# 784 more matmul pairs on zeros behind the warm-up of a two-block transformer kernel

## The chip, the cores and the metric

The kernel runs on one core of a Trainium2 chip. The metric is the device time of one execution in microseconds. Before the change the median of two runs is 2268.91 us (2268.64 to 2269.18).

## What is computed

The reference applies two transformer blocks, one after the other, to 256 tokens of width 2048, in float32. Cut to what matters:

```python
h = x
hn = rms_norm(h, norm_mix[i])
h = h + nsa_mixer(hn, nsa_w_in[j], nsa_w_out[j], ...)
hn = rms_norm(h, norm_ffn[i])
h = h + jnp.square(jax.nn.relu(hn @ ffn_w1[i])) @ ffn_w2[i]
gate = jax.nn.sigmoid(rms_norm(h, norm_ple[i]) @ ple_w_gate[i])
h = h + (p[i] @ ple_w_proj[i]) * gate
x = rms_norm(h, norm_final)
...
h = rms_norm_2(x, norm_g[i, 0])
m = swa_sink_attention(h, swa_w_in[j], swa_w_out[j], swa_sinks[j], rel_bias_table)
x = x + rms_norm_2(m, norm_g[i, 1])
h = rms_norm_2(x, norm_g[i, 2])
x = x + rms_norm_2(conv_ffn(h, ffn_w_up[i], ffn_conv[i], ffn_w_down[i]), norm_g[i, 3])
```

Nearly all of the work is products of the 256 tokens with weights, some 400 MB of them, each read once.

## The kernel before

The weights come as one stream of 128 x 128 blocks, in the order in which they are used. Class `Weights` loads 16 blocks (1 MB) at a time into one of three `w_raw` buffers (lines 216 to 231) and splits 8 blocks at a time into one of four `w_split` buffers (lines 233 to 249): ScalarE writes a rounded high part (line 243), VectorE the rest as a low part (line 244), both in the float32r type that TensorE takes in one pass. A load goes out when both halves of the buffer's last content are split, and a split into a buffer waits until TensorE has read what stood there.

A product to float32 accuracy is then three products of high and low parts. There are two forms of it. In `mm` (lines 297 to 303) the weight block is stationary: a matmul of the high part with 512 columns (the tokens' high and low parts side by side, line 302), then one of the low part with 256 columns (line 303). This is the pair that the change is about. In `mm_rows` (lines 316 to 325) the tokens are stationary, and 512 columns of weights stream past: three matmuls (lines 323, 324, 325) for each half of the tokens. Each matmul instruction loads its own stationary operand first; the trace has these loads as PEld.

All stationary operands of the float32r matmuls start at a multiple of 256 bytes within a partition; tiles named `pad` take up what is needed for that. The one exception is the warm-up's tile `idle`, which starts 224 bytes past such a multiple.

The program starts in `build` (from line 452): loads of the tokens and of the first weights, then a warm-up of nine matmuls of 512 columns on the zeros of `idle` (lines 485 to 489), whose output nobody reads. Then, for each of the 16 tiles of tokens, a split of the tile (line 500, done in lines 355 and 356) and its part of the first product (line 503, `mm_rows`); lines 543 and 544 follow with a second product of the same kind. The first `mm` is on line 554. The programs of the engines are written out in the order in which a tile framework's scheduler places them; it also sets the waits between engines. The engines are TensorE (PE), VectorE (DVE), ScalarE (ACT), GpSimd (POOL) and SyncE (SP, which issues the loads).

Of the kernel before, what the change touches and what calls it, by code (L numbers as in the profile page):

```python
# [8 lines left out]
F32 = mybir.dt.float32  # L9
F32R = mybir.dt.float32r  # L10
# [3 lines left out]
P = 128  # L14
S = 256
# [250 lines left out]
class Program:  # L266
# [185 lines left out]
    def build(self):  # L452
        tc, nc, ins = self.tc, self.nc, self.ins
        self.base = tc.alloc_tile_pool(name="base", bufs=1)
        self.psum = tc.alloc_tile_pool(name="psum", bufs=1, space=bass.MemoryType.PSUM)
        self.dram = tc.alloc_tile_pool(name="dram", bufs=1, space=bass.MemoryType.DRAM)
        self.pad(self.base, 64)
        self.w = Weights(nc, self.base, ins["w"], self.blocks)

        self.vecs = self.tile(self.base, [P, NV], F32, "vecs")  # L460
        cst = self.tile(self.base, [P, NC_], F32, "cst")
        self.ident = cst[:, C_ID : C_ID + P]
        self.ones = cst[:, C_ONE : C_ONE + P]
        self.fold = cst[:, C_FOLD : C_FOLD + 64]
        self.mask = cst[:, C_MASK : C_MASK + S]
        self.cmask = cst[:, C_CMASK : C_CMASK + 32].rearrange("p (b n) -> p b n", b=2)
        self.cvalid = cst[:, C_CVALID : C_CVALID + 32].rearrange("p (b n) -> p b n", b=2)

        self.eps = self.tile(self.base, [P, 1], F32, "eps")
        nc.vector.memset(self.eps, EPS)  # L470
        nc.scalar.dma_start(self.vecs[:, :KD], ins["vec"][:, :KD])
        self.x_pool = x_pool = tc.alloc_tile_pool(name="x0", bufs=1, side="right")
        x0 = [self.tile(x_pool, [P, 2, S], F32, f"x{i}") for i in range(KD // 2)]

        def load_x(i):
            nc.sync.dma_start(x0[i], ins["x"][:, 2 * i : 2 * i + 2])

        self.w.load(W_RAW, load_x)
        for i in range(2 * W_RAW, KD // 2):
            load_x(i)  # L480
        nc.scalar.dma_start(cst, ins["cst"])
        nc.scalar.dma_start(self.vecs[:, KD:], ins["vec"][:, KD:])


        idle = self.tile(x_pool, [P, COLS], F32R, "idle")
        nc.vector.memset(idle.bitcast(F32), 0.0)
        ps = self.ps_mm()
        for i in range(WARM):
            nc.tensor.matmul(ps, lhsT=idle[:, :P], rhs=idle, start=True, stop=True)


        xs = []
        acc = self.tile(x_pool, [P, S], F32, "acc")
        self.ps_vs = [self.ps_att(), self.ps_att()]
        for k in range(KD):
            src = x0[k // 2][:, k % 2]
            if k % 2 == 0:
                self.w.split(k // 2 + 1)
            x = self.slot(k, F32R)
            self.split512(x, src, self.vec(V_MIX + k))  # L500
            self.add_square(acc, src, k == 0)
            xs.append(x)
            self.mm_rows(self.ps_vs, [x], k == 0, k == KD - 1)
        self.pad(self.base, 96)
        self.nsa(xs, acc)
        self.ffn()
        self.ple()
        self.swa()
        self.conv_ffn()
        for pool in (self.pool_z, self.pool_y, self.dram, self.psum, self.base):  # L510
            pool.release()
        assert self.w.at == self.blocks

    def band_bias(self):

        nc, ins = self.nc, self.ins
        pool = self.tc.alloc_tile_pool(name="band", bufs=1)
        table = self.tile(pool, [BUCKETS, SWA_HEADS], F32, "table")
        hot = self.tile(pool, [BUCKETS, 2 * BANDP], F32, "hot")
        nc.sync.dma_start(table, ins["table"])  # L520
        nc.sync.dma_start(hot, ins["band"])
        ps = self.ps_att()
        nc.tensor.matmul(ps[:SWA_HEADS, :BANDP], lhsT=table, rhs=hot[:, :BANDP], start=True, stop=True)
        rows = self.tile(pool, [SWA_HEADS, BANDP], F32, "rows")
        nc.vector.tensor_tensor(rows, ps[:SWA_HEADS, :BANDP], hot[:, BANDP:], op=ALU.add)
        self.band = self.tile(self.dram, [SWA_HEADS, COPIES, BANDP], F32, "bandd")
        for c in range(0, COPIES, 16):
            nc.sync.dma_start(self.band[:, c : c + 16], rows[:, None, :].to_broadcast([SWA_HEADS, 16, BANDP]))
        pool.release()
# [690 lines left out]
```

## Time and profile before

| | |
|---|---|
| median of two runs | 2268.91 us |
| the profiled execution | 2269.81 us |
| its span, first to last instruction | 2268.0 us |
| PE busy | 2236.1 us (99%) |
| DVE busy | 1447.1 us (64%) |
| ACT busy | 1181.1 us (52%) |
| POOL busy | 243.2 us (11%) |
| HBM read | 410.03 MB |

The times of an instruction are those of the hardware's profiler. Matmuls are pipelined and their ends are modelled, so what one costs in a stream is read from the distance between starts, not from its duration. The granted clock is the share of TensorE's full clock that was granted. For the first 10 us the column of the clock prints full speed where the distances are those of half speed; there the distances are used.

### The profile page before, as it was taken

How to read it: one execution, taken by the hardware profiler on the slowest of the kernel's cores; microseconds unless marked ns; L12 is line 12 of the kernel's file. 1: busy time of each engine (PE TensorE's matmuls, PEld its weight loads, DVE VectorE, ACT ScalarE, POOL GpSimd, SP SyncE). 2: the span in 40 equal slices, each digit the busy share in tenths (PEclk: the TensorE clock that was granted, in tenths of full speed). 3: DMA queues.
4: the chain of work that ended last, by engine and by line, in shares of the span. 5: the costliest groups of instructions: out<-in, count | busy, mean ns of one | idle time of the engine just before them, and what ended most of it. 6: DMA issues, size and time to landing. Idle time of an engine off the chain costs nothing. (4 is left out here: it accounts for less than half of the span.)

```text
span 2268.0 us, 29986 instructions
## 1 busy us (share of the span) xinstructions
PE 2236.1 (99%) x11645; PEld 1892.5 (83%) x11645; DVE 1447.1 (64%) x2181; ACT 1181.1 (52%) x1894; POOL 243.2 (11%) x309
## 2 busy tenths in 40 slices
PE   8999999999999999999999999999999999999998
PEld 6888887888888888888888888778888888888886
DVE  7676665566544566644566777567756766765775
ACT  4566554444433444444465566456545544554554
POOL 5432210000000000000001123002100100110110
PEclk9999999999999999999999999999999999999999
DMA  6553335555555555555555544445555555555553
GB/s 254 196 199 127 123 128 213 185 201 186 196 192 191 197 186 187 186 186 188 212 191 185 204 142 165 167 147 189 187 195 189 188 186 186 186 189 200 186 186 130
DMA packets 65950, 415.64 MB, mean 183 GB/s; under 512 B 7408, under 2 KB 12528, under 8 KB 17424
## 3 DMA queue, kind: packets, MB, share of 16 engines
q1 hardware_dynamic: 65376, 413.01, 50.5%
q8 instruction: 91, 1.49, 0.2%
q10 hardware_dynamic: 432, 0.73, 0.1%
q14 instruction: 51, 0.42, 0.0%
HBM read 410.03 MB, written 3.67 MB: 182 GB/s over the span
## 5 line engine op out<-in xcount | busy, mean ns | idle before, releaser
L244 DVE TENSOR_TENSOR w_split<-w_raw,w_split 128x1024 fp32r<-128x1024 f32 (+1 forms) x759 | 946.4, 1248 | 641.9 <-ACT w_split L243 636.4
L243 ACT ACTIVATE w_split<-w_raw 128x1024 fp32r<-128x1024 f32 (+1 forms) x759 | 801.6, 1057 | 699.4 <-PE att L325 447.9
L302 PE MATMUL mm<-slot,w_split 128*128 128x512 f32 x3152 | 1117.3, 399 | 1.5 <-DVE z L346 1.5
L303 PE MATMUL mm<-slot,w_split 128*128 128x256 f32 x3152 | 885.2, 281 | 0.0
L302 PEld LDWEIGHTS mm<-slot,w_split 128*128 128x128 f32 x3152 | 592.0, 188 | 149.8 <-issue 3.4
L303 PEld LDWEIGHTS mm<-slot,w_split 128*128 128x128 f32 x3152 | 595.3, 189 | 0.3
L324 PE MATMUL att<-w_split,h 128*128 128x512 f32 x848 | 330.2, 389 | 0.0
L325 PE MATMUL att<-w_split,h 128*128 128x512 f32 x848 | 330.2, 389 | 0.0
L323 PE MATMUL att<-w_split,h 128*128 128x512 f32 x848 | 330.1, 389 | 0.0
L344 ACT ACTIVATE t<-mm 128x256 f32<-128x256 f32 x201 | 76.4, 381 | 228.5 <-PE mm L303 227.0
L325 PEld LDWEIGHTS att<-w_split,h 128*128 128x128 f32 x848 | 159.2, 188 | 33.1
L324 PEld LDWEIGHTS att<-w_split,h 128*128 128x128 f32 x848 | 159.2, 188 | 32.9
L323 PEld LDWEIGHTS att<-w_split,h 128*128 128x128 f32 x848 | 159.2, 188 | 32.8
L1107 POOL TENSOR_TENSOR u<-z,rb 128x256 f32<-128x256 f32 x88 | 71.0, 808 | 694.3 <-DVE z L346 585.3
L346 DVE TENSOR_TENSOR z<-mm,t 128x256 f32<-128x256 f32 x201 | 84.8, 423 | 79.8 <-ACT t L344 79.8
L324 PE MATMUL att<-w_split,slot 128*128 128x512 f32 x320 | 125.9, 393 | 4.0 <-DVE w_split L244 3.9
L323 PE MATMUL att<-w_split,slot 128*128 128x512 f32 x320 | 125.2, 393 | 1.8 <-ACT w_split L243 1.7
L325 PE MATMUL att<-w_split,slot 128*128 128x512 f32 x320 | 125.7, 393 | 0.0
L919 POOL MEMSET vh<- 128x512 f32 x1 | 0.5, 524 | 910.1 <-DVE sum L391 910.1
L324 PEld LDWEIGHTS att<-w_split,slot 128*128 128x128 f32 x320 | 60.4, 189 | 19.2 <-DVE w_split L244 6.8
L323 PEld LDWEIGHTS att<-w_split,slot 128*128 128x128 f32 x320 | 60.3, 189 | 15.1 <-ACT w_split L243 3.0
L325 PEld LDWEIGHTS att<-w_split,slot 128*128 128x128 f32 x320 | 60.4, 189 | 12.2
(261 smaller groups left out, 1901.0 us busy)
## 6 DMA issues: line engine op xcount, KB each, us to landing
w_raw<-in_w SPq DMA_DIRECT2D x376, 1024.0 KB, 4.8
bias<-bandd SPq DMA_DIRECT2D x32, 128.0 KB, 2.7
w_raw<-in_w SPq DMA_DIRECT2D x5, 512.0 KB, 7.6
x<-in_x SPq DMA_DIRECT2D x8, 256.0 KB, 6.9
slot<-in_xn SPq DMA_DIRECT2D x8, 256.0 KB, 7.9
gain<-in_rows SPq DMA_DIRECT2D x2, 1024.0 KB, 6.1
out<-slot SPq DMA_DIRECT2D x8, 256.0 KB, 2.0
bandd<-rows SPq DMA_DIRECT2D x2, 768.0 KB, 6.4
```

Of the source, the lines that this page charges most:

```text
L243: nc.scalar.activation(hi[:, c], raw[:, c], AF.Copy)
L244: nc.vector.tensor_tensor(lo[:, c], raw[:, c], hi[:, c].bitcast(F32), op=ALU.subtract)
L302: nc.tensor.matmul(ps, lhsT=hi, rhs=x, start=i == 0, stop=False)
L303: nc.tensor.matmul(ps[:, S:], lhsT=lo, rhs=x[:, :S], start=False, stop=i == n - 1)
L323: nc.tensor.matmul(ps[b], lhsT=xh, rhs=hi, start=first and i == 0, stop=False)
L324: nc.tensor.matmul(ps[b], lhsT=xh, rhs=lo, start=False, stop=False)
L325: nc.tensor.matmul(ps[b], lhsT=xl, rhs=hi, start=False, stop=last and i == n - 1)
L344: nc.scalar.activation(t, ps[:, S : 2 * S], AF.Copy)
L346: nc.vector.tensor_tensor(z, ps[:, :S], t, op=ALU.add)
L919: nc.gpsimd.memset(t[:, :, :, 64:128].bitcast(F32), 0.0)
L1107: nc.gpsimd.tensor_tensor(u[:, 2:], self.total(ps), rb, op=ALU.mult)
```

## The change

Behind the warm-up a function `probe` is called. It makes two tiles of zeros, `pa` with 1024 and `pc` with 512 columns, and issues 56 groups of 14 pairs. A pair has the two shapes of lines 302 and 303: 512 columns, then 256, each with a stationary operand of its own, the first cut from the left half of `pa`, the second from the right. Within a group both keep their place: `hi` and `lo` columns of four bytes past a multiple of 128 columns, so 0, 32, ... 224 bytes past a multiple of 512 (both tiles start at a multiple of 256 bytes in the built program). The groups run over all 56 pairs of different places. The multiple changes from pair to pair in a cycle of three. Nobody reads the output.

```diff
         for i in range(WARM):
             nc.tensor.matmul(ps, lhsT=idle[:, :P], rhs=idle, start=True, stop=True)
+        self.probe()
...
+    def probe(self):
+
+        nc = self.nc
+        pool = self.tc.alloc_tile_pool(name="probe", bufs=1)
+        a = self.tile(pool, [P, 1024], F32R, "pa")
+        c = self.tile(pool, [P, 512], F32R, "pc")
+        nc.vector.memset(a.bitcast(F32), 0.0)
+        nc.vector.memset(c.bitcast(F32), 0.0)
+        for hi in range(0, 64, 8):
+            for lo in range(0, 64, 8):
+                if hi == lo:
+                    continue
+                ps = self.ps_mm()
+                for i in range(14):
+                    at = P * (i % 3)
+                    nc.tensor.matmul(ps, lhsT=a[:, at + hi : at + hi + P], rhs=c, start=True, stop=True)
+                    at += 512
+                    nc.tensor.matmul(ps[:, :S], lhsT=a[:, at + lo : at + lo + P], rhs=c[:, :S], start=True, stop=True)
+        pool.release()
```

PE's queue at the program's start, before; the matmuls of lines 323 to 325 are those of the first product:

```order
L489 MATMUL mm_14_102<-idle_13_100 128x512 x9
L323 MATMUL att_16_113<-w_split0_115,slot0_18_120 128x512
L323 MATMUL att_17_114<-w_split0_115,slot0_18_120 128x512
L324 MATMUL att_16_113<-w_split0_115,slot0_18_120 128x512
L325 MATMUL att_16_113<-w_split0_115,slot0_18_120 128x512
```

The same with the change: the warm-up, the first pairs of the first group, and the last pairs of the last with what follows them.

```order
L489 MATMUL mm_14_102<-idle_13_100 128x512 x9
L530 MATMUL mm_17_119<-pc_16_116,pa_15_115 128x512
L532 MATMUL mm_17_119<-pc_16_116,pa_15_115 128x256
...
L530 MATMUL mm_72_1714<-pc_16_116,pa_15_115 128x512
L532 MATMUL mm_72_1714<-pc_16_116,pa_15_115 128x256
L323 MATMUL att_74_1745<-w_split0_1747,slot0_76_1752 128x512
L324 MATMUL att_74_1745<-w_split0_1747,slot0_76_1752 128x512
L325 MATMUL att_74_1745<-w_split0_1747,slot0_76_1752 128x512
```

All 1568 matmuls stand between the warm-up and the first product, and but for a few swapped neighbours in the first product PE's queue is unchanged behind them.

ACT's queue in the first product, before; `slot8` to `slot15` are tiles of tokens, `w_split4` is the fifth split of weights, the first that has to wait for a buffer that PE releases:

```order
L243 ACTIVATE w_split3_132<-w_raw1_86 128x1024 [waits DMAHW3_49]
L355 ACTIVATE slot8_33_238<-x4_9_76,vecs_2_64 128x256 [waits DMAHW4_49]
L355 ACTIVATE slot9_35_255<-x4_9_76,vecs_2_64 128x256
L243 ACTIVATE w_split4_161<-w_raw2_91 128x1024 [waits DMAHW5_49,DVE_49,PE_49]
L355 ACTIVATE slot10_37_267<-x5_10_77,vecs_2_64 128x256 [waits DMAHW6_49]
L355 ACTIVATE slot11_39_282<-x5_10_77,vecs_2_64 128x256
L243 ACTIVATE w_split5_188<-w_raw2_91 128x1024 [waits DMAHW7_49,DVE_49,PE_49]
```

The same with the change:

```order
L243 ACTIVATE w_split3_1764<-w_raw1_86 128x1024 [waits DMAHW3_49]
L355 ACTIVATE slot8_91_1870<-x4_9_76,vecs_2_64 128x256 [waits DMAHW4_49]
L355 ACTIVATE slot9_93_1887<-x4_9_76,vecs_2_64 128x256
L355 ACTIVATE slot10_95_1899<-x5_10_77,vecs_2_64 128x256 [waits DMAHW6_49]
L355 ACTIVATE slot11_97_1914<-x5_10_77,vecs_2_64 128x256
...
L355 ACTIVATE slot15_105_1970<-x7_12_79,vecs_2_64 128x256
L243 ACTIVATE w_split4_1793<-w_raw2_91 128x1024 [waits DMAHW5_49,DVE_49,PE_49]
L243 ACTIVATE w_split5_1820<-w_raw2_91 128x1024 [waits DMAHW7_49,DVE_49,PE_49]
```

The fifth and sixth split now stand behind all tiles of tokens, on ACT and in the same way on DVE. The queues of POOL and SP are unchanged.

## Rows read from the trace of the kernel before

**Rows 1.** The page's first part: busy time, share of the span, instructions.
```profile
PE 2236.1 (99%) x11645; PEld 1892.5 (83%) x11645; DVE 1447.1 (64%) x2181; ACT 1181.1 (52%) x1894; POOL 243.2 (11%) x309
```

**Rows 2.** PE's waits, 0 to 60 us: total us, times, longest.
```profile
PE att L324 <- DVE w_split L244: 3.9, 5, 1.7
PE att L323 <- ACT w_split L243: 1.7, 1, 1.7
```

**Rows 3.** Stretches of the start: busy us and instructions of each engine.
```profile
core 0: us, PE busy (x) PEld busy (x) DVE busy (x) ACT busy (x) POOL busy (x), PEclk, DMA share, GB/s
1.48:7.44 5.96, 4.21 (x10) 2.81 (x10) 0.51 (x2) 2.42 (x3) 1.18 (x2) 1.00 0.87 251
7.44:59.04 51.60, 47.52 (x196) 36.90 (x197) 39.92 (x35) 26.00 (x35) 32.61 (x29) 1.00 0.70 263
```

**Rows 4.** Line 489, the warm-up: ns min/median/max, first and last start in us.
```profile
L489 PEld LDWEIGHTS mm<-idle x9: 286/330/333, 1.5 to 4.6; 128*128 128x128 f32 x9
L489 PE MATMUL mm<-idle x9: 628/628/793, 1.5 to 5.1; 128*128 128x512 f32 x9
```

**Rows 5.** Timeline of PE from 7.4 us: start us, us, instruction, idle before.
```profile
7.44 1.22 PE L323 MATMUL att<-w_split,slot 128*128 128x512 f32 x2 [1.75 <-ACT w_split L243]
...
8.46 0.33 PEld L325 LDWEIGHTS att<-w_split,slot 128*128 128x128 f32 x1
8.88 0.63 PE L325 MATMUL att<-w_split,slot 128*128 128x512 f32 x1
9.31 0.63 PE L324 MATMUL att<-w_split,slot 128*128 128x512 f32 x1
...
10.16 0.47 PE L323 MATMUL att<-w_split,slot 128*128 128x512 f32 x1
10.47 0.40 PE L324 MATMUL att<-w_split,slot 128*128 128x512 f32 x1
10.70 0.40 PE L325 MATMUL att<-w_split,slot 128*128 128x512 f32 x1
```

**Rows 6.** Timeline of PE, 512-column matmuls in a row: first and last of seven.
```profile
700.50 0.39 PE L324 MATMUL att<-w_split,h 128*128 128x512 f32 x1
...
701.86 0.39 PE L324 MATMUL att<-w_split,h 128*128 128x512 f32 x1
```

**Rows 7.** Timeline of PE, end of the first two products.
```profile
58.68 0.50 PE L376 MATMUL att<-cst,acc 128*128 128x2 f32 x4
59.04 0.48 PE L302 MATMUL mm<-slot,w_split 128*128 128x512 f32 x1
```

**Rows 8.** Timeline of DVE, its first long instructions.
```profile
0.94 0.48 DVE L486 MEMSET idle<- 128x512 f32 x1
6.26 0.48 DVE L356 SCALAR_TENSOR_TENSOR slot<-x,vecs,slot 128x256 fp32r<-128x256 f32 x1 [4.83 <-ACT slot L355]
```

**Rows 9.** Timeline of PE, pairs of lines 302 and 303: first and eighteenth.
```profile
559.82 0.40 PE L302 MATMUL mm<-slot,w_split 128*128 128x512 f32 x1
...
565.83 0.40 PE L302 MATMUL mm<-slot,w_split 128*128 128x512 f32 x1
```

**Rows 10.** A stretch at the lower clock; the columns are those of rows 3.
```profile
1512.20:1519.00 6.80, 5.84 (x24) 5.37 (x25) 6.76 (x15) 3.15 (x8) 0.00 (x0) 0.50 0.01 2
```

**Rows 11.** Timeline of PE in that stretch: two pairs' first matmuls.
```profile
1517.27 0.63 PE L312 MATMUL mm<-slot,w_split 128*128 128x512 f32 x1
...
1517.91 0.63 PE L312 MATMUL mm<-slot,w_split 128*128 128x512 f32 x1
```

**Rows 12.** Timeline of PE, a change from 64 to 128 rows.
```profile
1288.18 0.28 PE L972 MATMUL att<-kt,q 64*128 64x256 f32 x1
1288.39 0.50 PE L302 MATMUL mm<-slot,w_split 128*128 128x512 f32 x1
1288.73 0.28 PE L303 MATMUL mm<-slot,w_split 128*128 128x256 f32 x1
```

## The prediction

> **What bounds the kernel now.** I read the page's first part, then the waits of TensorE (PE), then the stretches by engine, and only then single rows. The first part says that PE has a matmul in flight for 2236.1 of 2268.0 us, 99% of the span, VectorE (DVE) 64%, ScalarE (ACT) 52% [rows 1]. Of the waits of its first 60 us behind the warm-up there are only two kinds, 3.9 and 1.7 us, both for the split of the first weights [rows 2]. So the end is set by PE's own queue, instruction after instruction. A matmul put into that queue costs its own spacing, except where it falls into a stretch in which PE would have stood still. That leaves two questions: how much standing still there is at the place of the change, and how long one added pair takes.
>
> **The place.** The stretches show the start in two pieces [rows 3]: from 1.48 us the nine warm-up matmuls and a gap, and from 7.44 to 59.04 the first 192 real matmuls (two products of 96, lines 323 to 325). The added pairs stand in PE's queue between the ninth warm-up matmul and the first real one. The warm-up's last matmul starts at 5.1 us [rows 4], and at that clock one takes its 512 columns in 0.43 us (8.88 to 9.31 in the real ones [rows 5]), so a pair could start at 5.5 us. The first real matmul starts at 7.44, waiting for ACT [rows 5]: 1.94 us of cover.
>
> More cover lies behind. The 192 real matmuls and four small ones take 51.60 us [rows 3]. In a full stretch a 512-column matmul starts every 0.2267 us: 700.50 to 701.86 is six of them [rows 6]. 192 x 0.2267 = 43.53 us, and the four small ones of line 376 take 0.36 (58.68 to 59.04 [rows 7]). The remaining 7.71 us of the 51.60 are waits for the first weights and matmuls at the lower clock. After the pairs, hundreds of microseconds later, the first four split buffers, all sixteen activation tiles and the next three loads lie ready, so I take all of it as saved. Together the cover is 1.94 + 7.71 = 9.65 us.
>
> That ACT and DVE now split the activations before the fifth weight buffer, as the order shows, costs nothing: the fifth split waits for PE to release the first buffer. Behind it on ACT stand only further splits. PE eats one buffer in 12 x 0.2267 = 2.72 us and has four, so the fifth is wanted 8.2 us after it can be begun. If that cover were gone, a wait as long as the longest one now, 1.7 us [rows 2], would come back. The two new memsets on DVE follow that of the warm-up, which took 0.48 us for 512 columns [rows 8]. Three times that ends near 2.9 us, under the warm-up, and ahead of DVE's next work at 6.26 [rows 8]. Nothing else moves: SP's and POOL's queues are as they were, and so is every fixed address from the first projection on, but for buffers that rotate.
>
> **What one pair costs.** 56 groups of 14 are 784 pairs: one matmul of 512 columns and one of 256, each with weights of its own. The kernel has such pairs already, lines 302 and 303: from 559.82 to 565.83 us there are 17, so 0.3535 us a pair [rows 9]. All of their stationary operands start at place 0, a multiple of 256 bytes. In the probe the two start at two different places out of eight, 32 bytes apart. The trace before has no such pair at the full clock. So it has to be bounded.
>
> - From below: at the lower clock (granted 0.50, the level of 1.2 GHz) a pair takes 0.64 us: 1517.27 to 1517.91 [rows 10, 11]. There no overhead shows. Half of that, 0.320 us, is what the columns alone take at 2.4 GHz. 784 x 0.320 = 250.9 us.
> - From above: behind matmuls that use 64 rows, a 256-column one holds PE for 0.21 us (1288.18 to 1288.39) and the next 512-column one for 0.34 (to 1288.73) [rows 12]: 0.55 in place of 0.3535, as where a weight load isn't hidden. 784 x 0.55 = 431.2 us.
> - The only stationary that is off place in matmuls of this type is the warm-up's, 224 bytes past a multiple of 256 in the built program. At the lower clock its weight loads took 330 ns [rows 4], as the real ones did in the same stretch (0.33 [rows 5]), and no loss showed.
>
> Between ends far apart I take the row of the same two shapes at the same clock, 0.3535: 784 x 0.3535 = 277.1 us. The six 0.2267 rows (with 0.1133 for 256 columns, 0.340) would give 266.6.
>
> The Trainium skill, TensorE: Matmul & The Clock Gate, section Back-to-back issue gap, has a rule that speaks against this value: warm, a matmul starts columns / 2.4 + 2.5 ns after the one before. By it a pair is 325 ns and the sum 254.8 us. Here the trace doesn't agree: it has 227 ns [rows 6] where the rule has 216, and 353.5 [rows 9] where it has 325.
>
> **The clock.** The first pairs run at the lower level: the spacing is still 0.43 us at 9.31, and 0.23 from 10.47 on [rows 5]. PE did nothing from 5.5 to 7.44. With the pairs it is busy throughout, so I expect the rise between 5.5 and 10.3. Each microsecond at the lower level loses 1 - 0.3535/0.64 = 0.45 us: none to 2.15 us, I take 1.1.
>
> **The sum.** 277.1 + 1.1 - 9.65 = 268.6 us more. The profiled execution took 2269.81 us, span and what lies around it, 0.9 above the median of 2268.91, so the sum applies to either. On the median it gives 2537.5 us, 11.8% slower. About 2%, 45 us, is what a measurement of this kernel can tell from no change; the first 27 pairs (9.65 / 0.3535) are covered, and from some 155 on the loss passes 2%.
>
> **Rivals.**
> - *Off-place weights are dearer.* A load that starts between two multiples of 256 touches one stretch more, and the next matmul waits for it. For it: 33.5 ns of each pair are already more than its columns. Against: no loss in the warm-up, though only at the lower clock. With that overhead doubled a pair takes 0.387 us: 303.4 + 1.1 - 9.65 = 294.9, 2563.8 us. At the upper bound it is 422.7 more, 2691.6.
> - *Different places are cheaper.* The overhead comes from both loads falling on the same place, and goes where they differ. For it: loads of all kinds in the trace before share place 0, and all show overhead. Against: 512-column matmuls in a row have 13 ns of it and a pair 33.5, with the same places. With none left: 250.9 + 1.1 - 9.65 = 242.4, 2511.3 us. The page's rule named above would come out near there, at 2515.
> - *Zeros don't raise the clock.* For it: it rose 2.9 us after the first real matmul, and not in the warm-up's four microseconds. Against: the gap before 7.44 explains that as well. 784 x 0.64 = 501.8, less 9.65, with 1.4 for real matmuls that stay at the lower level: 493.6, 2762.5 us.
> - *Not slower: the pairs never run.* Nobody reads their output, so if they were dropped on the way to the chip, only two memsets are left, and the time is 2268.9. It decides as soon as fewer than 27 are left. Against: the nine warm-up matmuls are unread too, and all nine are in the trace [rows 4].
>
> **How the numbers follow.** The forecast (a pair between 0.335 and 0.370) has 0.68, dearer places 0.15, cheaper ones 0.10, no clock 0.05, no pairs 0.02. The range starts at 2511, where the columns alone are left, and ends at 2580, a pair of 0.407 us, past the doubled overhead; above it lie the clock and some 0.06 of the dearer places. All cases but the last are slower by over 2%: 0.98. The last is within 2%: 0.02.
>
> **What would show it.** In the profile after: lines 530 and 532 with 784 each, a pair every 0.35 us from some microsecond after 5.5, the first line 323 near 283.7 us, no wait on the w_split tile behind it, and the first line 302 about 43.9 us later, near 327.6; from there on everything 268.6 us later and no longer than before. The cost of the place is wrong if the spacing differs between groups, and then the groups tell which places. The cover is wrong if line 323 to 325 still waits for splits. The prediction is wrong at all if the stretch after the pairs is longer, which would be a cost of the pairs that I don't see here.

## The result, and the profile after

The changed kernel takes 2534.27 us (median of two runs, 2532.72 to 2535.82). The ratio to before is 1.1164, with a 95% interval of 1.1136 to 1.1192: 265.4 us more, where 268.6 were forecast. The profiled execution took 2535.82 us, its span is 2534.0.

The page's first part, after; it answers to [rows 1]:

```profile
PE 2509.4 (99%) x13213; PEld 2135.7 (84%) x13213; DVE 1444.6 (57%) x2183; ACT 1181.2 (47%) x1894; POOL 237.0 (9%) x309
```

PE has 1568 more instructions and 273.3 us more busy time. The other engines have the work they had, and DVE two memsets more. The groups by line show where PE's time came from. Columns: line, engine, operation, shapes, count, busy us, mean ns of one.

```profile
L530 PE MATMUL mm<-pc,pa 128*128 128x512 f32 x784 | 273.8, 394 | 0.0
L532 PE MATMUL mm<-pc,pa 128*128 128x256 f32 x784 | 219.6, 280 | 0.0
```

All 784 pairs ran. The two groups overlap, so their busy times don't add; the 273.8 us of the first is the stretch that the pairs fill. The stretches by engine, cut where the lines change, answer to [rows 3]:

```profile
1.48:5.45 3.97, 3.97 (x9) 3.14 (x10) 1.40 (x2) 1.17 (x1) 1.17 (x2) 1.00 0.83 205
5.45:279.19 273.74, 273.74 (x1569) 239.82 (x1568) 18.97 (x21) 11.42 (x22) 23.98 (x30) 1.00 0.07 27
279.19:323.15 43.96, 43.96 (x198) 36.41 (x197) 18.39 (x15) 16.08 (x16) 0.00 (x0) 1.00 0.46 160
```

The first column behind the bounds is the length, then busy us of PE, PEld, DVE, ACT and POOL. The warm-up and the pairs follow each other without a hole. In the third stretch the first two products take 43.96 us with PE busy all the time, where before they took 51.60 with PE busy for 47.52 [rows 3]. ACT's own waits show that the splits were ready long before:

```profile
ACT w_split L243 <- PE att L325: 286.3, 16, 261.4
```

One of its 16 waits for PE is 261.4 us long: the fifth split, for the buffer that PE releases behind the pairs. The timeline of PE at the two seams (start us, us, instruction):

```profile
4.64 0.98 PE L489 MATMUL mm<-idle 128*128 128x512 f32 x2
5.46 0.39 PE L530 MATMUL mm<-pc,pa 128*128 128x512 f32 x1
5.69 0.28 PE L532 MATMUL mm<-pc,pa 128*128 128x256 f32 x1
5.80 0.39 PE L530 MATMUL mm<-pc,pa 128*128 128x512 f32 x1
...
279.20 0.40 PE L323 MATMUL att<-w_split,slot 128*128 128x512 f32 x1
...
322.79 0.50 PE L376 MATMUL att<-cst,acc 128*128 128x2 f32 x4
323.15 0.48 PE L302 MATMUL mm<-slot,w_split 128*128 128x512 f32 x1
```

The first pair lasts from 5.46 to 5.80, at the upper clock level already. Line 302 first starts at 323.15 instead of 59.04 [rows 7]: 264.1 us later. The span has grown by 266.0, so 1.9 us come from what follows. PE's queue is the same there, so each of its instructions can be held against the same one before the change. Three things differ. First, the granted clock:

```profile
483.39:490.14 6.75, 6.75 (x24) 5.88 (x25) 5.01 (x28) 4.16 (x18) 1.16 (x3) 0.50 0.13 53
537.94:541.33 3.39, 3.39 (x12) 2.90 (x11) 2.26 (x15) 3.39 (x17) 0.00 (x0) 0.50 0.03 7
1695.15:1698.51 3.36, 3.36 (x10) 2.64 (x8) 1.02 (x2) 0.67 (x2) 0.00 (x0) 0.51 0.43 183
```

In these three stretches after the change the clock (third from the right) is 0.50 or 0.51. The same matmuls before the change had 1.00 in all three:

```profile
219.94:223.59 3.65, 3.65 (x24) 3.26 (x24) 3.39 (x20) 2.82 (x13) 0.00 (x0) 1.00 0.24 101
271.41:273.25 1.84, 1.84 (x12) 1.62 (x11) 1.83 (x13) 1.84 (x11) 0.00 (x0) 1.00 0.01 4
1428.47:1430.31 1.84, 1.84 (x10) 1.50 (x8) 1.02 (x2) 0.72 (x2) 0.00 (x0) 1.00 0.80 338
```

The same 24, 12 and 10 matmuls take 13.5 us and not 7.3. With their edges the three stretches push what follows back by 6.3 us.

Second, one of PE's waits before the change, near 347 us, is gone after it, which gives back 1.4:

```profile
PE mm L431 <- DVE slot L788: 1.7, 1, 1.7
```

Third, some of the kernel's own pairs start closer together. The longest such stream has 288 pairs; its first and last matmul of line 302, before and then after:

```profile
1555.21 0.47 PE L302 MATMUL mm<-slot,w_split 128*128 128x512 f32 x1 [1.50 <-DVE z L346]
1656.68 0.40 PE L302 MATMUL mm<-slot,w_split 128*128 128x512 f32 x1
1823.12 0.47 PE L302 MATMUL mm<-slot,w_split 128*128 128x512 f32 x1 [1.51 <-DVE z L346]
1922.68 0.40 PE L302 MATMUL mm<-slot,w_split 128*128 128x512 f32 x1
```

It takes 101.47 us before and 99.56 after. This and smaller differences give back 3.0 us together, and 6.3 - 1.4 - 3.0 = 1.9.

### The profile page after: what moved, and what is told of

It reads as the page before. It is cut to its first block, busy times and chain, and to the rows that moved or that the text cites. A ratio compares the mean times of both kernels' runs of the same rounds, so it can differ in the third digit from the quotient of the medians.

```text
span 2534.0 us, 33124 instructions
## 1 busy us (share of the span) xinstructions
PE 2509.4 (99%) x13213; PEld 2135.7 (84%) x13213; DVE 1444.6 (57%) x2183; ACT 1181.2 (47%) x1894; POOL 237.0 (9%) x309
## 5 line engine op out<-in xcount | busy, mean ns | idle before, releaser
L530 PE MATMUL mm<-pc,pa 128*128 128x512 f32 x784 | 273.8, 394 | 0.0
L532 PE MATMUL mm<-pc,pa 128*128 128x256 f32 x784 | 219.6, 280 | 0.0
L530 PEld LDWEIGHTS mm<-pc,pa 128*128 128x128 f32 x784 | 147.4, 188 | 34.0
L532 PEld LDWEIGHTS mm<-pc,pa 128*128 128x128 f32 x784 | 147.5, 188 | 0.1
```

Source lines behind the costliest of these rows:

```text
L530: nc.tensor.matmul(ps, lhsT=a[:, at + hi : at + hi + P], rhs=c, start=True, stop=True)
L532: nc.tensor.matmul(ps[:, :S], lhsT=a[:, at + lo : at + lo + P], rhs=c[:, :S], start=True, stop=True)
```

## The experiments

The question was where the 349.2 ns of a pair come from (273.74 us / 784), since the kernel's own pairs take 353.5 in the stretch of [rows 9] and 352.6 on average over its whole trace, and whether the cover behaved as reckoned. A group's distance is the mean over its last six steps from one pair's start to the next. Place 0 is a multiple of 256 bytes, and each place lies 32 bytes behind the one before; a group (2, 0) has its first stationary operand at place 2 and its second at place 0. In the changed kernel the distances run from 340.0 ns, in group (2, 0) alone, to 353.3, in (1, 4) and others.

**Both operands at one place.**

```diff
         for hi in range(0, 64, 8):
-            for lo in range(0, 64, 8):
-                if hi == lo:
-                    continue
+            for lo in [hi] * 7:
```

> The same 56 groups of 14 pairs, but both stationary operands of a pair at the same place, seven groups in a row for each of the eight places. Theory 'places decide': a pair at one place costs what the kernel's own pairs cost, 353.5 ns, so the pairs last 277.1 us and the whole about 2538 us. Rival 'the probe is cheaper anyway' (one moving tile, zeros, outputs written over): the pairs keep the changed kernel's mean of 349.2 ns, 273.7 us in all, and the whole stays at 2534 us.

Measured: 2536.04 us in one run, beside 2271.59 for the kernel before on that chip (median of 17, 2267.78 to 2274.01). The time of one run can't tell the two forecasts, 2538 and 2534, apart, since the kernel before spreads over 6 us on that chip; the distances can. Places 0 to 7 settle at 353, 353, 353, 347, 351, 350, 349 and 347 ns, and the pairs together take 275.3 us, between the 277.1 and 273.7 of the forecasts. Timeline of PE at place 0, then at place 3, first matmuls of pairs:

```profile
29.72 0.40 PE L528 MATMUL mm<-pc,pa 128*128 128x512 f32 x1
...
30.78 0.40 PE L528 MATMUL mm<-pc,pa 128*128 128x512 f32 x1
...
124.83 0.39 PE L528 MATMUL mm<-pc,pa 128*128 128x512 f32 x1
...
125.87 0.39 PE L528 MATMUL mm<-pc,pa 128*128 128x512 f32 x1
```

Three pairs take 1.06 us at place 0 and 1.04 at place 3. So at place 0 the probe's pair costs what the kernel's own does in [rows 9], zeros and unread output or not: the rival is out. But my theory was too simple as well: equal places aren't all alike.

**The groups in reverse order.**

```diff
-        for hi in range(0, 64, 8):
-            for lo in range(0, 64, 8):
+        for hi in range(56, -8, -8):
+            for lo in range(56, -8, -8):
```

> The same 56 groups in reverse order. Theory 'places decide': each pair of places keeps its spacing within 1 ns, (2, 0) stays the only one at 340.0 ns, and the sum stays 273.7 us. Rival 'what ran before decides': many groups move by 3 to 7 ns, (2, 0) is at 347 or 353 ns, and the sum may differ by a few us.

Measured: 2536.51 us, sum of the pairs 274.4 us. Group (2, 0) is at 340.0 again, and 46 of the 56 groups keep their value within 1 ns. Ten don't, so neither expectation holds as it stands; among the ten are these: (6, 0) goes from 350 to 340, (2, 5) from 353 to 347, (3, 1) from 352 to 343, (3, 6) from 348 to 353. Timeline of group (6, 0), after the change:

```profile
213.38 0.40 PE L530 MATMUL mm<-pc,pa 128*128 128x512 f32 x1
...
214.78 0.40 PE L530 MATMUL mm<-pc,pa 128*128 128x512 f32 x1
```

and in reverse order:

```profile
72.36 0.39 PE L530 MATMUL mm<-pc,pa 128*128 128x512 f32 x1
...
73.72 0.39 PE L530 MATMUL mm<-pc,pa 128*128 128x512 f32 x1
```

Four pairs in 1.40 us, and in 1.36. So places alone don't fix the distance: some groups have two rhythms. That what ran before picks one is likely, not shown. In the run with twice as many pairs, further down, the order is that of the change, and 52 of 56 groups keep their value; but two of the other four, (3, 7) and (7, 5), go from 346.7 to 353.3 behind the same groups as in the change. The sum hardly feels it. This run also has the lower clock over the first pairs:

```profile
5.49 0.63 PE L530 MATMUL mm<-pc,pa 128*128 128x512 f32 x1
...
6.13 0.63 PE L530 MATMUL mm<-pc,pa 128*128 128x512 f32 x1
...
7.34 0.39 PE L530 MATMUL mm<-pc,pa 128*128 128x512 f32 x1
```

The first pair takes 0.64 us, from about 7.3 on they take 0.35. That is the term that I had set at 1.1 us: here 0.8, in the changed kernel's trace none.

**Two groups only.**

```diff
-        for hi in range(0, 64, 8):
-            for lo in range(0, 64, 8):
+        for hi in (0,):
+            for lo in (8, 16):
```

> Two groups only, 28 pairs, places (0, 1) and (0, 2). Theory 'cover of 9.65 us': 28 x 0.347 = 9.7 us, nearly all of it in time in which PE waited or ran at the lower clock, so 2269 us, within 1.5 us of before. Rival 'no cover, each pair costs its spacing': 2278.6 us.

Measured: 2272.02 us, ratio 1.0006 (0.9996 to 1.0016), so 0.4 us more and not 9.7: most of the 28 pairs lie in cover. The stretches show that it isn't perfect so early:

```profile
5.45:15.17 9.72, 9.72 (x57) 8.54 (x56) 7.07 (x9) 7.18 (x14) 5.31 (x6) 1.00 1.03 404
15.17:60.58 45.41, 44.23 (x198) 36.33 (x197) 33.21 (x28) 20.01 (x25) 26.18 (x24) 1.00 0.63 230
```

The first two products take 45.41 us here and not 43.96, and PE stands still for 1.2 of it. The first line 302 starts 1.5 us later than before, so 8.2 of 9.72 us are covered. The timeline of DVE and PE around the wait:

```profile
25.30 3.35 DVE L356 SCALAR_TENSOR_TENSOR slot<-x,vecs,slot 128x256 fp32r<-128x256 f32 x4
28.57 8.23 DVE L244 TENSOR_TENSOR w_split<-w_raw,w_split 128x1024 fp32r<-128x1024 f32 x5
30.39 0.50 PE L324 MATMUL att<-w_split,slot 128*128 128x512 f32 x1 [1.18 <-DVE w_split L244]
```

PE waits for a split of weights, and DVE starts that split only when it is through with four tiles of tokens. The whole cover is there only when the probe is longer.

**Twice as many pairs in each group.**

```diff
-                for i in range(14):
+                for i in range(28):
```

> The 56 groups of the change with 28 pairs each. Theory 'each pair costs its spacing, and the cover counts once': 2268.9 + 2 x 273.7 - 9.65 = 2806.7 us, within 5 us. Rival 'a part of the loss is paid once, for filling PE's queue at the start': less than 273 us more than the changed kernel's 2534, below 2795.

Measured: 2807.2 us in one run, 0.5 from the forecast; from the kernel before on that chip, 2270.65 us in one run, it is 536.6 more, where 537.8 were forecast. Its two groups by line:

```profile
L530 PE MATMUL mm<-pc,pa 128*128 128x512 f32 x1568 | 548.0, 394 | 0.0
L532 PE MATMUL mm<-pc,pa 128*128 128x256 f32 x1568 | 439.3, 280 | 0.0
```

548.0 us for 1568 pairs is 349.5 ns each. The cost is linear and the cover counts once; nothing is paid for filling the queue.

**The kernel's own weights moved.** No probe; the high part of each split starts at place 2, the low part at place 0.

```diff
+ROOM = 2 * UNIT * P + 64
+AT_HI, AT_LO = 16, 1088
...
-            both = self.pool.tile([P, 2, UNIT * P], F32R, tag="w_split", name=f"w_split{u}", bufs=W_SPLIT)
-            hi, lo = both[:, 0], both[:, 1]
+            both = self.pool.tile([P, ROOM], F32R, tag="w_split", name=f"w_split{u}", bufs=W_SPLIT)
+            hi, lo = both[:, AT_HI : AT_HI + UNIT * P], both[:, AT_LO : AT_LO + UNIT * P]
...
-        diag = self.tmp("diag", 1, (P, 2, P))
+        diag = self.tmp("hz", 2).rearrange("p (b t) -> p b t", b=2)
```

> No probe. The kernel's own weights split so that the high part starts at place 2 (64 bytes past a multiple of 256) and the low part at place 0; the buffer is 64 columns longer, and a small diagonal tile shares the room of another. Theory 'places decide, (2, 0) is the cheap pair': the 3280 pairs of high and low weights go from 353.5 to 340 ns, 44 us less, about 2225 us, if the 512-column products that stream the shifted weights stay at 227 ns. Rival 'the 340 of group (2, 0) came from what ran before it': pairs at 349 to 353 ns, 2254 to 2269 us.

Measured: 2282.31 us, ratio 1.0048 (1.0034 to 1.0061): slower by half a per cent, and neither of the two forecasts. The pairs did get cheaper, 347.9 ns on average: 340 in some streams, 348 and 352 in turn in others, one rhythm from a stream's start to its end. But the three matmuls of `mm_rows`, where the weights stream past, went from 227 to 233 ns. The groups by line, here and to be held against [rows 6], where one takes 0.39:

```profile
L330 PE MATMUL att<-w_split,h 128*128 128x512 f32 x848 | 336.7, 397 | 0.0
L331 PE MATMUL att<-w_split,h 128*128 128x512 f32 x848 | 335.2, 395 | 0.0
L332 PE MATMUL att<-w_split,h 128*128 128x512 f32 x848 | 334.9, 395 | 0.0
```

4080 x 6.2 ns = 25 us lost, 3280 x 4.7 = 15 won. My condition that they stay at 227 failed.

**A grid of places**, for pairs and for the order of `mm_rows`.

```diff
+        for pw in range(0, 64, 8):
+            for px in range(0, 64, 8):
+                ps = self.ps_mm()
+                xs = x[:, px : px + 512]
+                for i in range(16):
+                    at = P * (i % 8) + pw
+                    nc.tensor.matmul(ps, lhsT=w[:, at : at + P], rhs=xs, start=True, stop=True)
+                    at += 1024
+                    nc.tensor.matmul(ps[:, S:], lhsT=w[:, at : at + P], rhs=xs[:, :S], start=True, stop=True)
...
+                        nc.tensor.matmul(ps, lhsT=xh, rhs=hi, start=True, stop=True)
+                        nc.tensor.matmul(ps, lhsT=xh, rhs=lo, start=True, stop=True)
+                        nc.tensor.matmul(ps, lhsT=xl, rhs=hi, start=True, stop=True)
```

> In place of the 56 groups: 64 groups of 16 pairs, both weights at one of eight places and the streamed tile at one of eight; then 64 groups of 24 matmuls of 512 columns in the order of lines 323 to 325, stationary at one of eight places and streamed weights at one of eight. Theory 'the distance between the places of stationary and streamed operand decides': the groups with the streamed tile at place 0 repeat 353, 352, 353, 347, 351, 350, 349, 347 ns for places 0 to 7, and at other places of the streamed tile the same row stands shifted. Rival 'the stationary's place alone decides': the same row at every place of the streamed tile. About 1024 x 0.350 + 1536 x 0.230 = 712 us of added matmuls by both, some 2970 us in all.

Measured: 2973.72 us in one run, beside 2270.65 before. Settled distances in ns, by the place of the streamed operand less that of the stationary one, modulo 8, the pairs' over the last six steps and those of `mm_rows` over the last twelve; each value is the same within 0.6 ns for all eight ways to have that distance, but for those noted:

```
distance             0      1      2      3      4      5      6      7
pair             353.3  346.7  353.3  350.0  351.1  346.7  353.3  353.3
one of mm_rows   226.7  233.3  228.9  233.3  233.3  234.2  233.3  233.3
pair, distance 0: 346.7 with both at place 0 or both at place 1
```

The first matmuls of two pairs twelve steps apart, with the weights at place 2: streamed tile at place 2, then at place 3.

```profile
107.74 0.40 PE L529 MATMUL mm<-px,pw 128*128 128x512 f32 x1
...
111.98 0.40 PE L529 MATMUL mm<-px,pw 128*128 128x512 f32 x1
...
113.37 0.39 PE L529 MATMUL mm<-px,pw 128*128 128x512 f32 x1
...
117.53 0.39 PE L529 MATMUL mm<-px,pw 128*128 128x512 f32 x1
```

Twelve pairs take 4.24 us at distance 0 and 4.16 at distance 1. The rows of the grid are one row shifted: the distance counts, not the place of the stationary alone. It doesn't settle everything. With all at place 0 a pair took 353.3 ns in the same-place run and takes 346.7 here. And place 6 had 349 there, where its distance, 2, has 353 here; the weights step through eight blocks here and through three there, and which difference between the two runs does it is open. The Trainium skill, TensorE: Matmul & The Clock Gate, section Step-by-step: what each phase is for, says that weight loads and the streamed operand have read ports of their own, and that a load takes no read bandwidth from the running matmul. The runs don't agree that the two are independent: where the one lies relative to the other moves a pair by up to 7 ns and a 512-column matmul by as much. Whether it is the reading in which they meet, no run here shows.

**Only the weights that are stationary in pairs moved**, first both parts to place 3 (distance 5), then high parts to place 2 and low parts to place 0, and a control with the new buffer, the shared diagonal tile and all at place 0. A string names for each part of the stream whether it is stationary (M) or streams past (R):

```diff
+AT = {'M': (16, 1088), 'R': (0, 1024)}
+KINDS = 'RRM' + 'MMMM' + 'MR' * 8 + 'MM' + 'M' * 18 + 'R' + 'MMRMR' + 'R' + 'RMMR' + 'MM' + 'MRM' * 3 + 'R'
...
+            hi, lo = (both[:, at : at + UNIT * P] for at in AT[UNIT_KINDS[u]])
```

With both at place 3, `'M'` is (24, 1048).

> No probe. Weights that are stationary in the pairs of 512 and 256 columns are split to place 3 (96 bytes past a multiple of 256), high and low part alike; weights that stream past stay at place 0. Theory 'the distance between the places of stationary and streamed operand decides': the 3280 pairs go from 352.6 to 346.7 ns and the 512-column products stay at 227, so 19 us less than before, a ratio of 0.9915. Rival 'the probe's spacing doesn't hold with real data and waits': 1.000 within 0.002.

> No probe. As the kernel with both at place 3, but the stationary high parts at place 2 and the low parts at place 0. Theory 'two rhythms, and what ran before picks one': pairs at 340 in some stretches and at 350 (348 and 352 in turn) in others, 347.9 ns on average as in the kernel that shifted all weights, the 512-column products back at 227: 15 us less than before, ratio 0.993, and anywhere from 8 to 41 us less. Rival 'place 2 was cheap only in the probe': 1.000 within 0.002.

> Control without probe: the longer weight buffer and the shared diagonal tile of the shifted kernels, but both parts at place 0. Theory: places alone made the difference, so this is as before, ratio 1.000 within 0.002, pairs at 352 to 353 ns. Rival 'the new layout itself costs': 1.003 to 1.005.

Measured, beside 2270.56 us before (median of 15): both at place 3, 2253.74 us, ratio 0.9931 (0.9918 to 0.9943); places 2 and 0, 2249.18 us, ratio 0.9906 (0.9893 to 0.9920); control 2273.09 us, ratio 1.0008 (0.9998 to 1.0017). The pairs' distances are 346.7, 343.6 and 352.4 ns, and the `mm_rows` matmuls are at 227 in all three. The groups by line for places 2 and 0:

```profile
L315 PE MATMUL mm<-slot,w_split 128*128 128x512 f32 x3152 | 1092.2, 393 | 1.3 <-DVE z L359 1.3
L337 PE MATMUL att<-w_split,h 128*128 128x512 f32 x848 | 330.3, 389 | 0.0
```

and for the control:

```profile
L309 PE MATMUL mm<-slot,w_split 128*128 128x512 f32 x3152 | 1118.2, 399 | 1.5 <-DVE z L353 1.5
L331 PE MATMUL att<-w_split,h 128*128 128x512 f32 x848 | 330.2, 389 | 0.0
```

With places 2 and 0, in a long stream, two first matmuls twelve pairs apart:

```profile
780.21 0.39 PE L315 MATMUL mm<-slot,w_split 128*128 128x512 f32 x1
...
784.29 0.39 PE L315 MATMUL mm<-slot,w_split 128*128 128x512 f32 x1
```

That is 340 ns a pair. Both versions beat the kernel before. At place 3 the gain is 16.8 us, short of the 19.4 that 3280 x 5.9 ns give, and the forecast ratio of 0.9915 lies just outside the interval; against the control, which has the same layout, the gain is 19.4. At places 2 and 0 the gain is 21 us and lies between the bounds of 8 and 41, with more pairs at 340 than forecast: two thirds in the profiled execution. Against the control's pairs 3280 x 8.8 ns are 28.9 us; the profiled execution is 28.3 below the control's profiled one and 24.4 below the median before. Its runs spread from 2246.12 to 2253.05, as a rhythm picked anew in each execution would make them; that isn't shown, with one trace of this kernel.

## Why the prediction was right

- **PE's queue sets the end, and a pair costs its spacing.** Right: 784 pairs fill 273.74 us, and twice as many 548.0.
- **277.1 us for the pairs.** 3.4 too much. The value came from the kernel's own pairs at 353.5 ns [rows 9]; the probe's average is 349.2, because its groups run from 340.0 to 353.3, as the places and the rhythm have it. The rival of cheaper places was right in its direction and far off in size: the overhead went from 33.5 to 29, not to nothing. The rival of dearer places is out: no group of the change settled above 353.3. That one row was taken for what a pair costs was weaker than it looked, for the trace before has other rows of the same two lines, with all stationary operands at place 0:

```profile
1260.09 0.39 PE L302 MATMUL mm<-slot,w_split 128*128 128x512 f32 x1
...
1264.25 0.39 PE L302 MATMUL mm<-slot,w_split 128*128 128x512 f32 x1
```

  Twelve pairs in 4.16 us are 346.7 ns each. From that row the pairs would have come to 271.8 us, 1.9 too little.
- **Lower clock, 1.1 us.** Mis-sized: none in this trace, where the first pair already runs at the upper level; 0.8 with the groups reversed, inside the bounds of 0 and 2.15. The rival that zeros don't raise the clock is out: it rose with PE on zeros alone.
- **Cover of 9.65 us.** Right: 5.46 + 273.74 + 43.95 - 59.04 = 264.11, so 9.63 were covered. Of these, 1.98 us lie ahead of the first real matmul and 7.65 in the first two products. With two groups alone 1.2 us of waiting stays, near the 1.7 that the prediction named for the case that the cover were gone.
- **Nothing else moves.** Right for the work, wrong for its time: 6.3 us were lost in three stretches at the lower clock, 1.4 came back with a wait that fell away and 3.0 with cheaper rhythms of the kernel's own pairs. The lower clock there doesn't need the probe. The control, which has none, shows it over part of the work of the second stretch (at 270.8 us) and of the third (at 1431.3 us):

```profile
270.80:274.20 3.40, 3.40 (x12) 2.94 (x12) 3.09 (x20) 2.86 (x13) 0.00 (x0) 0.50 0.18 75
```

  And 17 executions of the kernel before on one chip had mean granted clocks from 0.993 to 0.997 and times from 2267.78 to 2274.01 us.
- The errors have opposite signs: 268.6 - 3.4 - 1.1 + 1.9 = 266.0, the growth of the span. That they nearly cancel is luck, and the 1.9, itself a rest of larger terms, may come out otherwise in another execution.

## What to carry to other kernels

Work put into the queue of the engine that sets the end costs its spacing in a stream, taken from a row of the same shapes, less the time in which that engine stood still at that place. Matmuls whose operands look alike can differ by 4% with where the operands lie relative to each other in a partition, and by 2% in the same kernel from one stream to the next. So a row of the same shape is good to a few per cent, and several rows are better than one. If one tile is stationary in one product and streamed in another, each use may want a place of its own: moving it for both lost 11 us, moving it for one won 21.

## What the runs showed of the hardware that was not expected

- The spacing depends on the distance between the starts of stationary and streamed operand, modulo 256 bytes; it was measured in steps of 32 bytes: pairs from 346.7 to 353.3 ns with both weights at one place (at distance 0 either of the two), and 340.0 with the high part 64 bytes on. For 512-column matmuls of `mm_rows` equal places are best, 226.7 against 228.9 to 234.2.
- Some places have two rhythms, such as 340 and 350 ns, and a stream keeps the one that it falls into: in each of the eleven traces twelve streams of the kernel's own pairs, 31 to 512 pairs long, held one rhythm to their end. The kernel's own pairs at place 0 had 346.7 in some streams and 353.3 in others. What makes the loss, and what picks the rhythm, stays open.
- The granted clock fell to 0.50 in three stretches, 13.6 us together, whose work is the same in both kernels, in one trace and not in the other.
